# Order of work around an encoder's matmuls: operands, silu and residual ahead of weight casts, x turned between the first products, low parts on one engine

## The chip, the core and the metric

The kernel runs on one core of a Trainium2 chip. The core has five engines that run their own instruction queues in order: TensorE (PE, the matmuls and the transposes), VectorE (DVE), ScalarE (ACT), GpSimd (POOL) and SyncE (SP, here only the issuer of transfers). Operands lie in SBUF, products accumulate in PSUM, which has eight banks of 128 x 512 floats. The metric is the device time of one execution in microseconds (us).

## The reference

Two layers on x of 256 tokens by 1024 columns, all in float32. Each layer is

```python
x = x + 0.5 * swiglu(rms_norm(x, ffn1_norm[l]), ffn1_w_gate[l], ffn1_w_up[l], ffn1_w_down[l])
proj = rms_norm(x, mix_norm[l]) @ w_in[l]            # qa ka va qb kb vb, 2304 columns
out_a = windowed_gqa_sink(...)                       # 8 query heads, 2 key heads, ALiBi, sink
out_b = rms_norm(differential_attention(...), diff_subln[l]) * (1.0 - lam_init)
x = x + concat([out_a, out_b]) @ w_out[l]
x = x + 0.5 * swiglu(rms_norm(x, ffn2_norm[l]), ffn2_w_gate[l], ffn2_w_up[l], ffn2_w_down[l])
```

with `swiglu(h) = (silu(h @ w_gate) * (h @ w_up)) @ w_down` and 2816 hidden columns; a last RMSNorm ends it. All weights are read once, 167.5 MB of reads in the profile.

## The kernel before, in words

**Products in three parts.** A float32 product is made of three faster ones: every operand is split into a high part (rounded to float32r) and a low part (the rest), and high x high, low x high and high x low are added up in PSUM. So each weight tile is loaded to a buffer `raw` (SP issues the transfer), ACT writes the high part `whi` (line 106) and DVE the low part `wlo` (line 108). There are three buffers of each kind, and `weights()` starts the loads and casts of what comes two loads later (`LOOK = 2`). A load is 1 MB: 24 products of 512 columns use it. In the attention stage, from the fifth load of a layer on (`pooled`), the second half of each load's low parts is made by POOL instead of DVE. The products are lines 317 to 319 (`tokens`: the operand from x is the stationary side, 512 weight columns move) and 338 to 340 (`narrow`: the weights are stationary, 256 tokens move).

**Stages.** Each layer is feed-forward 1, attention, feed-forward 2. In a feed-forward the hidden columns come in five groups of 512 and one of 256. A group is a gate product and an up product (two loads each), `hidden` (silu of the gate on ACT, line 379, times up on DVE, line 384), `turn` (transposes on TensorE, line 398, then `split` into high on ACT, line 323, and low on DVE, line 324), and the product with the down weights, one group later. In the first group of a stage gate and up products alternate. In attention, `first_groups` makes the keys of the second head group, then come queries (`q_finish`), scores, softmax, transposes of the weights of attention, values, and the output projection.

**Between the stages.** `Residual.add` adds the result to x (`xk`, line 368) and takes the sum of squares on ACT (line 175). `Residual.turn(h)` turns half h of x: `Norm.pair` does four transposes (line 181) for two of the eight chunks of x and then two operands, high on ACT (line 185) and low on DVE (line 186). Half 0 is turned inside the last products of a stage, half 1 in `late()`, which the next stage calls in the middle of its first products. `stats` makes the factor of the norm from the sums of squares (DVE, POOL, DVE); it scales results, not operands, so that products can start without it. In the attention stage `spread` needs it, in the feed-forwards the silu.

**The start.** SP issues the four pieces of x in one queue with the pieces of the first two weight loads: x, two of each weight, x, two of each weight, x, x, and then the third load. `take_x` turns x in two halves, before the first and the second half of the first products.

**What orders the work.** The framework's scheduler orders each engine's instructions: of those that are ready in its model of time, the one written first goes first. A cast for the load after next is written before the products and operands of the present one, since `weights()` writes it, so it goes first where both are ready. On the chip each engine then keeps that order.

Of the kernel before, what the change touches and what calls it, by code (L numbers as in the profile page):

```python
# [33 lines left out]
def trunk(ctx: ExitStack, tc: tile.TileContext, x, n1, g1, u1, d1, nm, w_in, sink,  # L34
# [29 lines left out]


# [3 lines left out]
    pooled = set()  # L69
# [11 lines left out]
    def emit_load(i):  # L81
# [13 lines left out]
        for a, b in zip(cuts, cuts[1:]):  # L95
            if n == D:
                views = [(t[0][:, a:b, c:c + 512], t[1][:, a:b, c:c + 512], t[2][:, a:b, c:c + 512])
                         for t in [(raw, hi, lo)] for c in (0, 512)]
            elif i not in paired:
                views = [(raw[:, a:b], hi[:, a:b], lo[:, a:b])]  # L100
            else:
                views = [(raw.rearrange("p k (s c d) -> p c k s d", s=2, c=2)[:, c, a:b],
                          hi.rearrange("p k (c s d) -> p c k s d", s=2, c=2)[:, c, a:b],
                          lo.rearrange("p k (c s d) -> p c k s d", s=2, c=2)[:, c, a:b]) for c in range(2)]
            for r_, h_, l_ in views:
                act.copy(h_, r_)  # L106
                eng = pool if i in pooled and a in cuts[2:] else dve
                eng.tensor_tensor(l_, r_, f(h_), op=ALU.subtract)  # L108
            if i < 2:
                yield  # L110
# [11 lines left out]
    for l in range(DEPTH):  # L122
# [28 lines left out]
        pooled.update(range(mixed + 4, len(specs)))  # L151
# [14 lines left out]
    class Norm:  # L166
# [6 lines left out]
        def squares(self, t, c, n):  # L173
            j_ = tmp("junk", 2, (P, 512))
            self.last = act.activation(j_[:, :n], xk[:, t, c:c + n], AF.Square, accum_out=self.ss[:, t, c // 256:c // 256 + 1])

        def pair(self, j):
            sl = halves(bank())
            for i in range(2):
                for t in range(2):  # L180
                    pe.transpose(sl[:, i, t * P:(t + 1) * P], xk[:, t, (2 * j + i) * P:(2 * j + i + 1) * P], ident)
            xs = blk()
            for i in range(2):
                g = gcol[:, self.g0 + 2 * j + i:self.g0 + 2 * j + i + 1]
                act.activation(xs[:, i, 0:S], sl[:, i], AF.Identity, scale=g)  # L185
                dve.scalar_tensor_tensor(xs[:, i, S:512], in0=sl[:, i], scalar=g, in1=f(xs[:, i, 0:S]),  # L186
                                         op0=ALU.mult, op1=ALU.subtract)
# [27 lines left out]
    for j in range(4):  # L215
        sp.dma_start(xk[:, :, j * 256:(j + 1) * 256], x[0].rearrange("(t p) d -> p t d", p=P)[:, :, j * 256:(j + 1) * 256])
        for e in early * 2 if j < 2 else ():
# [142 lines left out]
    class Residual:  # L360
# [5 lines left out]
        def add(self, h, t):  # L366
            xv = xk[:, t, h * 512:(h + 1) * 512]
            dve.tensor_tensor(xv, xv, self.accs[h][t], op=ALU.add)
            self.nxt.squares(t, h * 512, 512)

        def turn(self, h):
            for j in (2 * h, 2 * h + 1):
                self.nxt.pair(j)

    def ffn(norm, aside=None, before=None, final=False):
        def gate(acc, t):
            g = tmp().rearrange("p a n -> p (a n)")
            n = acc.shape[1]
            act.activation(g[:, :n], acc, AF.Silu, scale=norm.r[:, t:t + 1])  # L379
            return g[:, :n]  # L380

        def up(h, acc, g, t):
            n = acc.shape[1]
            dve.scalar_tensor_tensor(h[:, t, :n], in0=acc, scalar=norm.hr[:, t:t + 1], in1=g, op0=ALU.mult, op1=ALU.mult)  # L384
# [7 lines left out]
        def turn(hs, n):  # L392
            out_ = []
            for i in range(n):
# [5 lines left out]
                split(hb, sl)  # L400
# [51 lines left out]
    def ffn_close(parts, nxt):  # L452
# [11 lines left out]
        def late():  # L464
            res.turn(1)
            nxt.stats()
        nxt.late = late

    def mix(l, norm, nxt_norm):
# [15 lines left out]
        def q_finish(sl, sc):  # L485
            t = tmp()
            q = tp.tile([P, 2, 512], F32R, tag="q", bufs=3, name=nm_("q"))
            for i in range(2):
                dve.scalar_tensor_tensor(t[:, i], in0=sl[:, i], scalar=sc[i], in1=norm.R, op0=ALU.mult, op1=ALU.mult)
            split(q, t)  # L490
# [118 lines left out]
        oa = [bank() for _ in range(2)]  # L609
# [10 lines left out]
        for h in range(HB):  # L620
            for t in range(2):
                j_ = tmp("junk", 2, (P, P))
                act.activation(j_, osl[t][:, h * P:(h + 1) * P], AF.Square, accum_out=ss[:, t, h:h + 1])
        d1 = den_b.rearrange("p h (t a) -> p a t h", a=2)[:, 0]
        dd = tmp("dd", 1, (P, 2, HB))
        dve.scalar_tensor_tensor(dd, in0=d1, scalar=EPS, in1=d1, op0=ALU.mult, op1=ALU.mult)
        dve.scalar_tensor_tensor(ss, in0=ss, scalar=1.0 / P, in1=dd, op0=ALU.mult, op1=ALU.add)
        rb = tmp("rb", 1, (P, 2, HB))
        pool.tensor_tensor(rb.rearrange("p t h -> p (t h)"), ss.rearrange("p t h -> p (t h)"), mhalf, op=ALU.pow)
        on = blk(F32)  # L630
        for t in range(2):
            dve.tensor_tensor(on[:, t].rearrange("p (h d) -> p h d", h=HB), osl[t].rearrange("p (h d) -> p h d", h=HB),
                              rb[:, t].unsqueeze(2).to_broadcast([P, HB, P]), op=ALU.mult)
# [18 lines left out]
        for hp, src in enumerate(turned(on)):  # L652
            dst = oT[2 + hp]
            act.activation(dst[:, :, 0:S], src, AF.Copy, scale=gsub[:, l:l + 1])
            dve.scalar_tensor_tensor(dst[:, :, S:512], in0=src, scalar=gsub[:, l:l + 1], in1=f(dst[:, :, 0:S]),
                                     op0=ALU.mult, op1=ALU.subtract)
# [28 lines left out]
        def late():  # L685
            res.turn(1)
            nxt_norm.stats()
        nxt_norm.late = late
# [93 lines left out]
```

## Time and profile before

| | before |
|---|---|
| median of three runs | 998.27 us (995.05 to 998.62) |
| the profiled execution | 997.01 us, span 995.2 us |
| TensorE busy | 961.8 us, 97% of the span |
| DVE, ACT, POOL busy | 550.0, 476.7, 53.6 us |
| mean granted TensorE clock | 0.991 |
| traffic | 169 GB/s over the span |

In the listings a line gives the start in us from the span's start, the length in us, engine, line of the kernel, operation, tile written and tiles read, shape and count; in brackets the idle time of the engine ahead of it and what ended that. In the waits a line gives the waiting engine and line, what it waited for, the total in us, how often and the longest. In the stretches each engine has its busy time and, in brackets, its instructions; then come the granted clock, the share of the DMA engines and GB/s. A busy TensorE is not one at its peak: lengths of neighbouring matmuls overlap, and the distance of their starts tells more.

### The profile page before, as it was taken

To read this page: it belongs to the slowest core of one execution; us is meant where nothing else is said; L and a number is where in the kernel's file an instruction comes from. 1 tells how busy PE (TensorE), PEld (TensorE's weight loads), DVE (VectorE), ACT (ScalarE), POOL (GpSimd) and SP (SyncE) were. 2 spreads that over 40 slices of the span, in tenths; PEclk is the share of its full clock that TensorE was granted. 3 is DMA by queue.
4 is the path that set the end of the run, shared out by engine and by line. 5 is a ranking of instruction groups with operands and counts; after the bars stand their busy time and mean duration, and the time that the engine had idled before them with its cause. 6 is when DMAs were issued, how large, how long until landed. Compare 5 with 4: busy or idle time off the path is not lost.

```text
span 995.2 us, 12394 instructions
## 1 busy us (share of the span) xinstructions
PE 961.8 (97%) x4940; PEld 813.7 (82%) x4940; DVE 550.0 (55%) x816; ACT 476.7 (48%) x809; POOL 53.6 (5%) x78
## 2 busy tenths in 40 slices
PE   6999999999999999999999999999999999999996
PEld 5788888889798788888878888887988887888885
DVE  4645454568945555454555545456597455454553
ACT  5544443457745443434445343435477355444433
POOL 4000000004100000000000000000230000000001
PEclk9999999999999999999999999999999999999999
DMA  8655565635515555656545565555445245565531
GB/s 264 212 195 186 174 206 173 204 97 182 150 43 169 178 202 172 196 182 200 181 143 194 172 209 170 192 188 184 118 142 152 85 169 169 190 212 187 195 127 42
DMA packets 98218, 169.39 MB, mean 170 GB/s; under 512 B 3182, under 2 KB 30896, under 8 KB 98160
## 3 DMA queue, kind: packets, MB, share of 16 engines
q1 hardware_dynamic: 97872, 168.31, 51.3%
q0 software_dynamic: 288, 0.30, 0.4%
q8 instruction: 38, 0.62, 0.2%
q14 instruction: 20, 0.16, 0.0%
HBM read 167.54 MB, written 1.05 MB: 169 GB/s over the span
## 4 chain that ended last, share of the span: by engine, by line
PE 90%; DVE 3%; ACT 3%; issue 2%; DMA 2%; SPq 0%; POOLq 0%; POOL 0%; ACTq 0%; DVEq 0%
PE ps L317 25%; PE ps L318 25%; PE ps L319 25%; PE ps L398 2%; PE ps L338 2%; PE ps L339 2%; PE ps L340 2%; DMA raw<-in_ffn_w_up_dram 2%; PE ps L615 1%; DVE wlo L108 1%; ACT whi L106 1%; PE ps L567 1%; PE ps L502 1%; ACT s L512 1%; PE ps L588 1%
## 5 line engine op out<-in xcount | busy, mean ns | idle before, releaser
L108 DVE TENSOR_TENSOR wlo<-raw,whi 128x1024 fp32r<-128x1024 f32 (+2 forms) x364 | 375.8, 1076 | 338.0 <-ACT whi L106 336.1
L106 ACT CAST whi<-raw 128x1024 fp32r<-128x1024 f32 (+2 forms) x392 | 323.2, 882 | 356.0 <-PE ps L318 322.4
L317 PE MATMUL ps<-whi,s 128*128 128x512 f32 x1126 | 433.2, 393 | 6.2 <-ACT s L185 5.3
L318 PE MATMUL ps<-whi,s 128*128 128x512 f32 x1126 | 439.0, 390 | 0.0
L319 PE MATMUL ps<-wlo,s 128*128 128x512 f32 x1126 | 437.0, 390 | 0.0
L317 PEld LDWEIGHTS ps<-whi,s 128*128 128x128 f32 x1126 | 211.8, 189 | 49.7 <-ACT s L185 5.8
L318 PEld LDWEIGHTS ps<-whi,s 128*128 128x128 f32 x1126 | 212.6, 189 | 43.8 <-DVE s L186 0.5
L319 PEld LDWEIGHTS ps<-wlo,s 128*128 128x128 f32 x1126 | 212.3, 189 | 43.5
L338 PE MATMUL ps<-s,whi 128*128 128x256 f32 x224 | 64.8, 293 | 4.3 <-ACT s L185 4.3
L339 PE MATMUL ps<-s,whi 128*128 128x256 f32 x224 | 64.9, 290 | 0.0
L340 PE MATMUL ps<-s,wlo 128*128 128x256 f32 x224 | 64.4, 288 | 0.0
L379 ACT ACTIVATE tmp<-ps,r 128x512 f32<-128x512 f32 (+1 forms) x48 | 31.2, 651 | 62.9 <-PE ps L319 62.8
L384 DVE SCALAR_TENSOR_TENSOR s<-ps,hr,tmp 128x512 f32<-128x512 f32 (+1 forms) x48 | 32.7, 705 | 41.2 <-PE ps L319 24.7
L338 PEld LDWEIGHTS ps<-s,whi 128*128 128x128 f32 x224 | 43.5, 196 | 5.6 <-ACT s L185 4.8
L339 PEld LDWEIGHTS ps<-s,whi 128*128 128x128 f32 x224 | 44.3, 198 | 0.1
L340 PEld LDWEIGHTS ps<-s,wlo 128*128 128x128 f32 x224 | 44.3, 198 | 0.0
L196 POOL TENSOR_TENSOR r<-ms,mhalf 128x2 f32<-128x2 f32 x6 | 4.2, 706 | 637.7 <-DVE ms L194 637.7
L512 ACT ACTIVATE s<-s,negm 128x256 f32<-128x256 f32 x64 | 31.8, 499 | 12.4 <-DVE negm L510 12.3
L324 DVE TENSOR_TENSOR s<-ps,s 128x512 fp32r<-128x512 f32 x48 | 31.0, 684 | 8.2 <-ACT s L323 8.2
L108 POOL TENSOR_TENSOR wlo<-raw,whi 128x256 fp32r<-128x256 f32 (+1 forms) x28 | 31.7, 1156 | 62.4 <-ACT whi L106 62.4
L323 ACT CAST s<-ps 128x512 fp32r<-128x512 f32 x48 | 25.7, 583 | 12.1 <-PE ps L398 9.7
L398 PE MATMUL ps<-ident,s 128*128 128x128 f32 x176 | 24.7, 274 | 4.3 <-DVE s L384 4.3
(115 smaller groups left out, 456.4 us busy)
## 6 DMA issues: line engine op xcount, KB each, us to landing
raw<-in_ffn_w_down_dram SPq DMA_DIRECT2D x44, 1024.0 KB, 4.9
raw<-in_ffn_w_gate_dram SPq DMA_DIRECT2D x39, 1024.0 KB, 5.0
raw<-in_ffn_w_up_dram SPq DMA_DIRECT2D x39, 1024.0 KB, 5.0
raw<-in_w_in_dram SPq DMA_DIRECT2D x14, 1024.0 KB, 5.1
raw<-in_ffn_w_gate_dram SPq DMA_DIRECT2D x8, 512.0 KB, 3.7
raw<-in_ffn_w_up_dram SPq DMA_DIRECT2D x8, 512.0 KB, 4.7
raw<-in_w_in_dram SPq DMA_DIRECT2D x8, 512.0 KB, 4.6
raw<-in_w_out_dram SPq DMA_DIRECT2D x4, 1024.0 KB, 4.8
```

Source lines behind the costliest of these rows:

```text
L106: act.copy(h_, r_)
L108: eng.tensor_tensor(l_, r_, f(h_), op=ALU.subtract)
L317: pe.matmul(accs[t], lhsT=xh, rhs=hi[:, k], start=kk == first, stop=False)
L318: pe.matmul(accs[t], lhsT=xl, rhs=hi[:, k], start=False, stop=False)
L319: pe.matmul(accs[t], lhsT=xh, rhs=lo[:, k], start=False, stop=kk == (last if isinstance(last, int) else last[t]))
L338: pe.matmul(acc, lhsT=wh, rhs=xv[:, 0:S], start=first and i == 0 and j == 0, stop=False)
L339: pe.matmul(acc, lhsT=wh, rhs=xv[:, S:512], start=False, stop=False)
L340: pe.matmul(acc, lhsT=wl, rhs=xv[:, 0:S], start=False, stop=last and i == len(kcs) - 1 and j == 1)
L379: act.activation(g[:, :n], acc, AF.Silu, scale=norm.r[:, t:t + 1])
L384: dve.scalar_tensor_tensor(h[:, t, :n], in0=acc, scalar=norm.hr[:, t:t + 1], in1=g, op0=ALU.mult, op1=ALU.mult)
L398: pe.transpose(sl[:, c, t * P:(t + 1) * P], hs[:, t, (2 * i + c) * P:(2 * i + c + 1) * P], ident)
L512: act.activation(e[:, t, c], e[:, t, c], AF.Exp, scale=-1.0, bias=negm[:, n:n + 1], accum_out=den[:, n:n + 1])
```

## The change

`urgent()` puts the instructions written inside it 300 places earlier in the order that the scheduler goes by. It is put around the operands of a norm (`Norm.operands`), the residual add, silu and the multiply with up, the split of the turned hidden block and the finish of the queries. The casts of weights do not get it.

The sums of squares leave `add` and follow `turn`, without priority. `late` gets a step number: the second half of x is turned after the first 24 products of a stage (one quarter of the 256-column products, the first half of the first pair of loads), before it was after the first half of all; the statistics come one step later. In a feed-forward's first group the second half of the gate product is finished before the second half of the up product. In the second group the turn of the first hidden block comes after the first 24 products of the gate.

At the start ACT's queue issues the four pieces of x, one after every two pieces of weights as written; x is turned in four steps between products, and the sums of squares of x queue behind the operands on ACT. The block that writes the attention constants was queued behind the last sum of squares on ACT and is now queued behind the last operand on DVE.

In attention the norm of the second head group (`norm_b`) with its transposes is written ahead of the last quarter of the first head group's products, before it was behind them. No low part of a weight is made on POOL any more: 28 operations of POOL, 12 of 512 and 16 of 256 columns, go to DVE.

```diff
+    def urgent():
+        return tc.high_priority(300)
...
-                eng = pool if i in pooled and a in cuts[2:] else dve
-                eng.tensor_tensor(l_, r_, f(h_), op=ALU.subtract)
+                dve.tensor_tensor(l_, r_, f(h_), op=ALU.subtract)
...
-            self.last = act.activation(j_[:, :n], xk[:, t, c:c + n], AF.Square, accum_out=...)
+            act.activation(j_[:, :n], xk[:, t, c:c + n], AF.Square, accum_out=...)
...
+            with urgent():
+                self.operands(j, sl)
+
+        def operands(self, j, sl):
             xs = blk()
             for i in range(2):
                 g = gcol[:, self.g0 + 2 * j + i:self.g0 + 2 * j + i + 1]
-                act.activation(xs[:, i, 0:S], sl[:, i], AF.Identity, scale=g)
-                dve.scalar_tensor_tensor(xs[:, i, S:512], ...)
+                self.last_act = act.activation(xs[:, i, 0:S], sl[:, i], AF.Identity, scale=g)
+                self.last = dve.scalar_tensor_tensor(xs[:, i, S:512], ...)
...
     for j in range(4):
-        sp.dma_start(xk[:, :, j * 256:(j + 1) * 256], ...)
-        for e in early * 2 if j < 2 else ():
+        act.dma_start(xk[:, :, j * 256:(j + 1) * 256], ...)
+        for e in early:
             next(e)
...
     def take_x(k):
-        if k < 2:
-            for j in (2 * k, 2 * k + 1):
-                norm.pair(j)
-                for e in early * 2 if k == 0 else ():
-                    next(e)
+        if k < 4:
+            norm.pair(k)
+            for e in early * 2 if k < 2 else ():
+                next(e)
         else:
-            for t in range(2):
-                for h in range(2):
-                    norm.squares(t, h * 512, 512)
+            with tc.issue_after(norm.last_act.ins):
+                for t in range(2):
+                    for h in range(2):
+                        norm.squares(t, h * 512, 512)
+            norm.stats()
...
         for k in range(0, KC, 2):            # first_groups
-            if k == 4:
-                norm.late()
+            if k:
+                norm.late(k // 2 + 1)
...
         def add(self, h, t):
             xv = xk[:, t, h * 512:(h + 1) * 512]
-            dve.tensor_tensor(xv, xv, self.accs[h][t], op=ALU.add)
-            self.nxt.squares(t, h * 512, 512)
+            with urgent():
+                dve.tensor_tensor(xv, xv, self.accs[h][t], op=ALU.add)
 
         def turn(self, h):
             for j in (2 * h, 2 * h + 1):
                 self.nxt.pair(j)
+            for t in range(2):
+                self.nxt.squares(t, h * 512, 512)
+
+        def late(self, k):
+            if k == 2:
+                self.turn(1)
+            elif k == 3:
+                self.nxt.stats()
...
-        for k0 in (0, 4):                    # ffn, first group
-            if before is not None:
-                before(k0 // 4)
-            elif k0 == 4:
-                norm.late()
-            ws = (weights(), weights())
-            for k in (0, 2):
-                for sl, w in zip((gs, us), ws):
-                    tokens(sl, norm.xs, w, k0, (k, k + 1))
-        if before is not None:
-            before(2)
-            norm.stats()
+        if before is None:
+            before = norm.late
+        before(0)
+        ws = (weights(), weights())
+        for k in (0, 2):
+            before(k // 2 + 1)
+            for sl, w in zip((gs, us), ws):
+                tokens(sl, norm.xs, w, 0, (k, k + 1))
+        before(3)
+        for sl in (gs, us):
+            tokens(sl, norm.xs, weights(), 4)
+        before(4)
         h = hidden(gs, us)
         for g in range(1, NGRP):
-            hT = turn(h, 2)
-            gs, us = [bank(), bank()], [bank(), bank()]
-            for sl in (gs, us):
-                for k0 in (0, 4):
-                    tokens(sl, norm.xs, weights(), k0)
+            if g > 1:
+                hT = turn(h, 2)
+            gs = [bank(), bank()]
+            tokens(gs, norm.xs, weights(), 0)
+            if g == 1:
+                hT = turn(h, 2)
+            tokens(gs, norm.xs, weights(), 4)
+            us = [bank(), bank()]
+            for k0 in (0, 4):
+                tokens(us, norm.xs, weights(), k0)
...
+            with urgent():                   # q_finish; likewise gate, up, split in turn
+                for i in range(2):
+                    dve.scalar_tensor_tensor(t[:, i], in0=sl[:, i], scalar=sc[i], in1=norm.R, ...)
+                split(q, t)
...
         for t in range(2):
             for c in range(4):
+                if (t, c) == (1, 2):
+                    norm_b()                 # the block below, and turned(on) with its operands
                 for a in range(2):
                     for kc in range(2):
                         pe.matmul(oa[t][...], lhsT=pT[c][...], rhs=vA[...], ...)
-        ss = tmp("ss", 1, (P, 2, HB))
-        ... squares of osl, mean, pow on POOL, on = osl * rb
-        for hp, src in enumerate(turned(on)):
-            ...
```

More of the change, by code (lines that the diff above doesn't have):

```diff
@@ L68, in trunk @@
     paired = set()
-    pooled = set()
     fine = {2, 3}
@@ L378, in gate @@
             n = acc.shape[1]
-            act.activation(g[:, :n], acc, AF.Silu, scale=norm.r[:, t:t + 1])
+            with urgent():
+                act.activation(g[:, :n], acc, AF.Silu, scale=norm.r[:, t:t + 1])
             return g[:, :n]
@@ L383, in up @@
             n = acc.shape[1]
-            dve.scalar_tensor_tensor(h[:, t, :n], in0=acc, scalar=norm.hr[:, t:t + 1], in1=g, op0=ALU.mult, op1=ALU.mult)
+            with urgent():
+                dve.scalar_tensor_tensor(h[:, t, :n], in0=acc, scalar=norm.hr[:, t:t + 1], in1=g, op0=ALU.mult, op1=ALU.mult)
         def hidden(gs, us):
@@ L399, in turn @@
                 hb = blk()
-                split(hb, sl)
+                with urgent():
+                    split(hb, sl)
                 out_.append(hb)
@@ L462, in ffn_close @@
             res.add(1, t)
[L464 to L467, printed above, removed]
+        nxt.late = res.late
     def mix(l, norm, nxt_norm):
@@ L487, in q_finish @@
             q = tp.tile([P, 2, 512], F32R, tag="q", bufs=3, name=nm_("q"))
-            for i in range(2):
-                dve.scalar_tensor_tensor(t[:, i], in0=sl[:, i], scalar=sc[i], in1=norm.R, op0=ALU.mult, op1=ALU.mult)
-            split(q, t)
+            with urgent():
+                for i in range(2):
+                    dve.scalar_tensor_tensor(t[:, i], in0=sl[:, i], scalar=sc[i], in1=norm.R, op0=ALU.mult, op1=ALU.mult)
+                split(q, t)
             return [q[:, 0], q[:, 1]]
@@ L616, in mix @@
                                   rhs=vA[:, kc, a * 64:a * 64 + 64], start=kc == 0, stop=kc == 1)
-        ss = tmp("ss", 1, (P, 2, HB))
[L620 to L633, printed above, removed]
         ra = tmp("ra", 1, (P, 4, 4))
@@ L683, in mix @@
             res.add(1, t)
[L685 to L688, printed above, removed]
+        nxt_norm.late = res.late
     fss = const.tile([P, 2, 4], F32, name="fss")
```

48 lines of the change are left out of this document (32 added, 16 removed).

## The prediction

> **What bounds the kernel now.** I read the page first, then the time listing of TensorE, then the waits, the listings of ACT, DVE and POOL around each TensorE hole, and last the stretches with their granted clock.
>
> ```profile
> PE 961.8 (97%) x4940; PEld 813.7 (82%) x4940; DVE 550.0 (55%) x816; ACT 476.7 (48%) x809; POOL 53.6 (5%) x78
> PE 90%; DVE 3%; ACT 3%; issue 2%; DMA 2%; SPq 0%; POOLq 0%; POOL 0%; ACTq 0%; DVEq 0%
> ```
>
> TensorE is the chain; nothing in the change takes work from it. In the listing 512-column products start 0.2275 us apart (140.03, 140.26, 140.49), 256-column ones 0.12, transposes 0.109. The middle of each feed-forward stage runs at that distance without a hole. So only time that neighbouring starts stand apart beyond this can be won. Added up over the trace, such excess is some 33 us net, and most of it lies in a dozen places. The waits say on whom:
>
> ```profile
> PEld ps L317 <- ACT s L185: 5.8, 2, 3.6
> PEld ps L338 <- ACT s L185: 4.8, 2, 2.4
> PEld ps L502 <- DVE q L324: 4.5, 2, 2.2
> PE ps L398 <- DVE s L384: 4.3, 4, 1.6
> ```
>
> Three of the four are products waiting for their own operands from ACT or DVE, and the fourth is the transpose of the hidden block waiting for silu times up. What ACT does meanwhile, at the start of the first attention stage (eight transposes began at 202.90, the product waits until 206.09):
>
> ```profile
> 202.87 1.66 ACT L106 CAST whi<-raw 128x512 fp32r<-128x512 f32 x3
> 204.44 0.62 ACT L175 ACTIVATE junk<-xk 128x512 f32<-128x512 f32 x1
> 204.97 0.18 ACT L175 ACTIVATION_READ_ACCUMULATOR junk<-xk 128x1 f32 x1
> 205.06 0.60 ACT L106 CAST whi<-raw 128x512 fp32r<-128x512 f32 x1
> 205.57 0.46 ACT L185 ACTIVATE s<-ps,gcol 128x256 fp32r<-128x256 f32 x1
> ```
>
> Four casts of a load two ahead and a sum of squares stand before the operand. Behind such a hole the clock falls:
>
> ```profile
> 25.80:29.30 3.50, 3.29 (x7) 2.32 (x8) 3.50 (x9) 2.77 (x5) 0.00 (x0) 0.51 0.96 304
> 204.00:208.00 4.00, 1.92 (x11) 1.92 (x12) 3.87 (x10) 3.73 (x11) 0.71 (x1) 0.85 0.40 129
> 208.00:212.00 4.00, 4.00 (x28) 4.00 (x27) 2.33 (x8) 1.63 (x4) 0.00 (x0) 0.73 0.92 250
> 252.00:256.00 4.00, 2.13 (x19) 1.80 (x17) 4.00 (x5) 3.33 (x7) 2.95 (x2) 1.00 0.00 0
> 504.00:508.00 4.00, 4.00 (x17) 3.53 (x16) 3.00 (x8) 2.24 (x6) 0.62 (x1) 0.61 0.79 262
> ```
>
> The last but one number before the bandwidth is the granted clock, ahead of the DMA share. From 206.8 to 210.2 starts are about twice as far apart (0.215 for 0.12): 3.4 us at half speed loses 1.7. The same follows the holes at 22, 500 and 691, not the one at 253.
>
> **The change part by part.** The profiled execution took 997.0 us (span 995.2), 1.3 below the median 998.3; the sum is made against 997.0.
>
> *Operands first, second half of x turned after the first products, residual add first.* Stages start badly three times: holes of 2.31 (203.7), 2.13 (500.5) and 2.31 (691.3), each with 1.7 of half clock behind it: 6.75 + 5.1 = 11.9. With priority the operand (0.46 on ACT, 0.48 on DVE) starts when its transposes end, and the adds no longer stand behind low parts (200.79 for three adds, after 2.36 of low parts). Turning the first half then fits under the twelve last products of the stage, 2.7. The second half comes after 24 products, 2.9 (256 columns) or 5.5 us (512); the last add, 0.69, and a transpose fit under that. Nearest row for a well covered start: the second feed-forward, 311 to 317, with 0.2 of excess. Bounds: an operand still behind one cast (1.05) leaves about 1.3 of each hole and the clock drop, gain 2.7; all of it, 11.9. I take 11.9 less 3 x 0.2 = **11.3**. The sums of squares lose their early place: 2 x 0.8 on ACT, then DVE, POOL (0.70) and DVE, in all some 3 us, needed at the end of the first group 11 us later, so nothing; without that cover it would be those 3 us per stage.
>
> *Start of the kernel.* x leaves SP's queue for ACT's: four issues of 0.44 to 0.62, 2 us, stand before ACT's table load (1.28) and its first cast at 4.19, so 0.7 + 2 + 1.28 just fits; bound a loss of 0.5. SP's ninth weight issue moves up by the four it loses. The last x piece was issued at 6.3 and landed 11.6 later; now it goes some 4 us sooner. The constants' DVE work (four operations, 2.2 us, 8.87 to 13.4) now queues behind the last DVE operand. The hole after the transposes at 21.6 is 3.54, then 1.7 of half clock: 5.2. Weights allow it: the third load's first low part ends at 21.9, and the fourth load's at 27.4, where its products would begin at 22.5 + 24 x 0.2275 = 27.9. An operand made on the spot costs 0.3. Bounds: 4.4 (late ACT) to 6.3 (first product at 7 instead of 9.15: five half-clock products, 1.1). I take **4.9**.
>
> *Gate finished before up, the next group's first 24 products before the turn.* Silu now follows the gate half, 24 products = 5.5 us before up ends; table load, two silus and two multiplies are 1.28 + 2 x 0.69 + 2 x 0.74 = 4.1, and another 5.5 us of products lie before the transposes. So these holes go: 1.03 (38.4), 0.46 (527), 1.74 (334.9) and 1.74 (822.5), **5.0**. Bounds 3 to 5. PSUM holds: silu frees the gate's two banks before the next two are asked for.
>
> *q first, no low parts on POOL.* The hole at 253.9 (2.18; again 2.19 at 741):
>
> ```profile
> 251.97 2.97 POOL L108 TENSOR_TENSOR wlo<-raw,whi 128x512 fp32r<-128x512 f32 x2 [6.67 <-ACT whi L106]
> 252.36 3.13 DVE L108 TENSOR_TENSOR wlo<-raw,whi 128x512 fp32r<-128x512 f32 x2
> 255.42 0.68 DVE L324 TENSOR_TENSOR q<-tmp,q 128x512 fp32r<-128x512 f32 x1
> ```
>
> q's low part waits behind two weight low parts that take 3.13 beside POOL, while two took 1.28 at 256.8 without it. Priority removes the hole; then DVE is the danger. POOL's work per layer becomes 8 x 0.36 + 6 x 0.64 = 6.7 us on DVE; overlap with POOL had cost DVE 5.5 there (2.06 at 242.5, 1.85 at 252.4, the rest at 224, 229 and 233). Net 1.2 into a stretch, 220 to 264, in which DVE was busy 39.9 of 44. Bounds: without the relief 6.7 - 4.1 idle = 2.6 lost per layer; with all, 2.2 won. I take half the hole, 2 x 1.2 = **2.4**, because the softmax operations right behind have no priority.
>
> *Norm of the second head group before the last quarter of the first group's products.* The hole at 287.9 (0.61, twice) is the output projection waiting for ACT's 0.70. The normed block ends at 285.4, three quarters of the 64 products at 280.2 + 5.3 = 285.5; the last 16 (1.8 us) cover the operand. **1.2**; bounds 0 and 1.2.
>
> Sum: 11.3 + 4.9 + 5.0 + 2.4 + 1.2 = 24.8; 997.0 - 24.8 = **972.2**.
>
> **The rivals.**
>
> *Half of it: the wait is passed on.* Behind operands stand the casts, behind q the softmax, and the cores run in order: an operand caught behind one running cast of 1.05 keeps the clock drop. Stage starts 2.7 to 5, start 3, gates 4, q nothing, norm 0.6: about 13, 984. For it: DVE busy 39.9 of 44. Against: the second feed-forward's start works with the same helper.
>
> *The clock still drops.* The half-clock stretches stay though the holes go: the stage starts give 3 x 1.7 = 5.1 less, 977. For it: a hole of 2.2 us cost clock at 203 and none at 253. Against: every stretch begins within 5 us of a hole that follows eight transposes (0.87), and the hole at 253 follows none. [...]
>
> *The order does not change*, because the scheduler had nothing else ready, or the operands were already first. Then 997. Against: the listing shows casts ahead of operands that were ready.
>
> *Slower: casts lose their lead.* An urgent silu, split or add set early into ACT's or DVE's queue waits for TensorE, and the casts behind it wait too. It costs nothing while a cast keeps its lead: a cast freed at 140.7 has its low part at 144.1, and its products begin at about 152.3, 8 us later. It decides from the point where each of the 24 groups of the four feed-forwards loses 24.8 / 24 = 1.0 us, that is, where casts come 9 us late; at 10 us late, 24 x 2 = 48 less 24.8, about 1020. Against: in the middle of a stage ACT sits idle 2.5 to 4 us before nearly every pair of casts.
>
> **How the numbers follow.** Forecast (966 to 976) 0.54; clock still drops (977) 0.06; half of it (980 to 988) 0.22; order unchanged 0.06; slower 0.08; better, with the first product and q at their upper bounds, 997.0 - 28.2 = 969 and less, 0.04. The range runs from 965, a little under that bound, to the far end of the half case, 988; the rest leaves it with 0.06 + 0.08 and a few hundredths. A measurement of this kernel tells about 0.5%, 5 us, from no change. Faster by more: 0.54 + 0.06 + 0.22 + 0.04 = 0.86; same 0.06; slower 0.08.
>
> **What would show it.** Right: no product waiting over 0.5 us for an operand of line 185 at the three stage starts, granted clock 1.00 in all stretches after the start, transposes of the hidden block directly behind products, first group done near 33 instead of 38, no POOL low parts, DVE near 550 + 13.4 - 11 = 552 busy. Wrong: products waiting for the casts or low parts of weights, the spreading product waiting for late squares, DVE without idle time around 250, a half-clock stretch that stays.

## The result and the profile after

| | before | after |
|---|---|---|
| median (four runs each) | 998.03 us (995.05 to 998.62) | 979.51 us (978.32 to 980.62) |
| ratio after / before | | 0.9821, 95% interval 0.9804 to 0.9837 |
| the profiled execution | 997.01 us, span 995.2 | 978.65 us, span 976.8 |
| mean granted TensorE clock | 0.991 | 0.996 |

The change saves 18.4 us in the profiled executions, where 24.8 were forecast; 972.2 was the forecast, inside a range of 965 to 988. The size is near, but one large term failed and two others came out differently. Lines of the kernel have moved: 185 is now 190 (operand, high part), 186 is 191, 181 is 182 (transposes of x), 106 and 108 are 109 and 110 (cast and low part), 317 to 319 are 323 to 325, 338 to 340 are 344 to 346, 398 is 415.

The page after, busy time and the shares of the chain that ended last:

```profile
PE 954.5 (98%) x4940; PEld 809.3 (83%) x4940; DVE 549.9 (56%) x844; ACT 475.7 (49%) x809; POOL 21.2 (2%) x50
PE 95%; DMA 2%; ACT 2%; issue 0%; DVE 0%; SPq 0%; POOLq 0%; POOL 0%; ACTq 0%
```

DVE took POOL's 28 low parts and is no busier (549.9 for 550.0). The waits of TensorE after, total in us, how often, longest:

```profile
PE ps L233 <- DMA grow<-in_ffn_norm_dram: 6.5, 1, 6.5
PE ps L344 <- ACT s L190: 4.3, 2, 2.1
PE ps L323 <- ACT s L190: 2.0, 1, 2.0
PE ps L323 <- ACT s L658: 0.9, 2, 0.5
PE ps L628 <- ACT v L617: 0.6, 2, 0.3
```

The wait for silu times up and the wait for q are gone. The three waits for the first operand of a stage (line 190) are not. The fourth row is the one that was to go with the norm of the second head group, and the fifth is new.

Where the 18.8 us up to the last product came from is read by setting the starts of the same TensorE operations (the landmarks) in the two traces against each other. Each row is the change of that difference over a stretch.

| stretch, by its ends | after minus before, us | the prediction's term |
|---|---|---|
| start to the hidden block's transposes in group two (73.31, now 66.02) | -7.29 | start -4.9, first gate -1.03 |
| the three later first groups of feed-forwards: 309.88 to 370.51, 499.77 to 561.3, 797.51 to 858.14 | -1.83, -0.54, -1.83 | gates -1.74, -0.46, -1.74 |
| attention stages' starts to first scores (202.90 to 232.15; 690.56 to 719.77) | -1.49, -1.45 | stage starts, with the one at 500: -11.3 |
| first scores to products of the second head group (to 276.5; to 764.12) | -2.76, -2.80 | q -2.4 |
| from there to the next transposes of x (309.88; 797.51) | +0.50, +0.73 | norm -1.2 |

The loss in the last row does not come from the move of the norm, as two of the experiments below show: all but 0.2 of it comes with POOL's low parts going to DVE. So it belongs with the row above it, and the two together are -4.3 over both layers.

**The stage starts.** ACT after, at the first attention stage (start, length, line, operation, tiles, shape, count):

```profile
194.86 0.61 ACT L176 ACTIVATE junk<-xk 128x512 f32<-128x512 f32 x1
195.59 2.18 ACT L109 CAST whi<-raw 128x512 fp32r<-128x512 f32 x4
197.68 0.62 ACT L176 ACTIVATE junk<-xk 128x512 f32<-128x512 f32 x1
198.30 0.45 ACT L190 ACTIVATE s<-ps,gcol 128x256 fp32r<-128x256 f32 x1
```

TensorE beside it:

```profile
195.62 1.03 PE L182 MATMUL ps<-ident,xk 128*128 128x128 f32 x8
198.81 0.51 PE L344 MATMUL ps<-s,whi 128*128 128x256 f32 x2 [2.15 <-ACT s L190]
```

It is the picture of before: four casts and a sum of squares stand ahead of the operand. The excess between neighbouring starts is 2.31 (196.4), 2.13 (487.7) and 2.31 (677.9), to 10 ns the three holes of before. What the stages won, 1.5 each, is a half-clock stretch that no longer follows the first and the third hole; it still follows the second:

```profile
491.20:494.60 3.40, 3.40 (x13) 2.92 (x12) 2.84 (x8) 2.16 (x6) 0.61 (x1) 0.50 0.90 282
677.90:682.00 4.10, 1.95 (x17) 1.71 (x16) 3.98 (x10) 4.10 (x12) 0.56 (x1) 1.00 0.53 176
```

The number ahead of the DMA share is the granted clock: 0.50 behind the hole of 2.13, 1.00 through the longer hole of 2.31.

**The queries.** DVE after, at the place where two low parts had taken 3.13 beside POOL:

```profile
245.76 2.49 DVE L110 TENSOR_TENSOR wlo<-raw,whi 128x512 fp32r<-128x512 f32 x4
248.17 0.68 DVE L330 TENSOR_TENSOR q<-tmp,q 128x512 fp32r<-128x512 f32 x1
```

Four low parts in 2.49 are 0.62 each, for 1.57 each before. q still stands behind them; they are only shorter, and TensorE runs from product to product.

**The second head group.** TensorE after, around the end of attention:

```profile
265.86 3.39 PE L628 MATMUL ps<-v,s 128*128 128x128 f32 x28 [0.28 <-ACT v L617]
269.09 7.03 PE L670 MATMUL ps<-vA,s 128*128 128x64 f32 x62
275.96 0.39 PE L635 MATMUL ps<-ident,s 128*128 128x128 f32 x2
276.36 0.82 PE L635 MATMUL ps<-ident,s 128*128 128x128 f32 x6
277.63 1.19 PE L323 MATMUL ps<-whi,s 128*128 128x512 f32 x4 [0.45 <-ACT s L658]
```

`norm_b` is written ahead of the last 16 of the 64 products of the first head group (line 670), but 62 of them went ahead of its transposes (line 635), so that nothing covers the operand (line 658) and its hole of 0.61 stays. A new hole stands ahead of the second head group's values. ACT there, after:

```profile
262.49 0.67 ACT L617 ACTIVATE v<-ps,r 128x512 f32<-128x512 f32 x1
263.05 2.17 ACT L109 CAST whi<-raw 128x512 fp32r<-128x512 f32 x4
265.13 0.68 ACT L617 ACTIVATE v<-ps,r 128x512 f32<-128x512 f32 x1
```

And before, the same three steps of ACT and the products that read the values:

```profile
273.39 0.69 ACT L596 ACTIVATE v<-ps,r 128x512 f32<-128x512 f32 x1 [0.31 <-PE ps L590]
273.97 2.17 ACT L106 CAST whi<-raw 128x512 fp32r<-128x512 f32 x4
276.05 0.68 ACT L596 ACTIVATE v<-ps,r 128x512 f32<-128x512 f32 x1
276.50 3.74 PE L607 MATMUL ps<-v,s 128*128 128x128 f32 x32
```

In both, the second copy of the values waits behind four casts; the order is an old one. Before, the copy ended at 276.73, 0.23 after the first of the products. Now it ends at 265.81, 0.84 after the first (264.97), because TensorE, no longer held up ahead of q, comes sooner. So the products that read it (line 628) have a hole of 0.45 (0.50 in the second layer).

### The profile page after: what moved, and what is told of

Read it like the earlier page. It is cut to its first block, busy times and chain, and to the rows that moved or that the text cites. A ratio compares the mean times of both kernels' runs of the same rounds, so it can differ in the third digit from the quotient of the medians.

```text
span 976.8 us, 12379 instructions
## 1 busy us (share of the span) xinstructions
PE 954.5 (98%) x4940; PEld 809.3 (83%) x4940; DVE 549.9 (56%) x844; ACT 475.7 (49%) x809; POOL 21.2 (2%) x50
## 4 chain that ended last, share of the span: by engine, by line
PE 95%; DMA 2%; ACT 2%; issue 0%; DVE 0%; SPq 0%; POOLq 0%; POOL 0%; ACTq 0%
PE ps L323 26%; PE ps L324 26%; PE ps L325 26%; PE ps L344 3%; PE ps L345 3%; PE ps L346 3%; PE ps L415 2%; DMA raw<-in_ffn_w_gate_dram 2%; PE ps L670 1%; PE ps L523 1%; ACT whi L109 1%; PE ps L609 1%; PE ps L610 1%; PE ps L611 1%; PE ps L628 1%; PE ps L182 1%
## 5 line engine op out<-in xcount | busy, mean ns | idle before, releaser
L344 PE MATMUL ps<-s,whi 128*128 128x256 f32 x224 | 63.3, 287 | 4.3 <-ACT s L190 4.3
L345 PE MATMUL ps<-s,whi 128*128 128x256 f32 x224 | 63.6, 285 | 0.0
L344 PEld LDWEIGHTS ps<-s,whi 128*128 128x128 f32 x224 | 42.4, 191 | 5.3 <-ACT s L190 4.8
L345 PEld LDWEIGHTS ps<-s,whi 128*128 128x128 f32 x224 | 42.9, 192 | 0.2
L190 ACT ACTIVATE s<-ps,gcol 128x256 fp32r<-128x256 f32 x48 | 20.7, 472 | 7.4 <-PE ps L182 4.1
L415 PEld LDWEIGHTS ps<-ident,s 128*128 128x128 f32 x176 | 20.7, 140 | 3.2
```

The costliest lines, as they stand in the source:

```text
L344: pe.matmul(acc, lhsT=wh, rhs=xv[:, 0:S], start=first and i == 0 and j == 0, stop=False)
L345: pe.matmul(acc, lhsT=wh, rhs=xv[:, S:512], start=False, stop=False)
L415: pe.transpose(sl[:, c, t * P:(t + 1) * P], hs[:, t, (2 * i + c) * P:(2 * i + c + 1) * P], ident)
```

## The experiments

The kernel before has a median of 996.7 us beside the first four runs (12 runs of it) and 996.5 beside the last four (7 runs). Holes are, as in the prediction, the excess of the distance between two neighbouring starts.

**The first casts and the squares queued behind the stage's operands.** The changed kernel, with an order written out on ACT in both kinds of stage:

```diff
-        ws = (weights(), weights())
+        with tc.issue_after(norm.last_act.ins):
+            ws = (weights(), weights())
...
-            for t in range(2):
-                self.nxt.squares(t, h * 512, 512)
+            with tc.issue_after(self.nxt.last_act.ins):
+                for t in range(2):
+                    self.nxt.squares(t, h * 512, 512)
```

> The changed kernel, with the casts of the first loads of a stage and the sums of squares queued on ACT behind the high parts of the operands of the first half of x (an order edge, no wait). Theory A, the holes at the stage starts stayed because four casts and a sum of squares still stand ahead of the operand in ACT's queue: the holes of 2.31, 2.13 and 2.31 us shrink to about 0.6 each, the half-clock stretch behind the second one goes (1.7), 3 x 1.6 + 1.7 = 6.5 us less than the changed kernel, 973. Rival B, the operand is late because the closing products of both halves end together and the residual adds come last: the holes stay above 1.5, and the time is 977 to 980.

Measured 971.29 us (970.69 to 971.76), 0.9736 of before (0.9719 to 0.9753): 8.2 below the changed kernel. ACT and TensorE of this kernel at the first attention stage:

```profile
196.01 0.84 ACT L190 ACTIVATE s<-ps,gcol 128x256 fp32r<-128x256 f32 x2 [4.21 <-PE ps L182]
```

```profile
195.69 0.60 PE L182 MATMUL ps<-ident,xk 128*128 128x128 f32 x4
196.53 0.51 PE L344 MATMUL ps<-s,whi 128*128 128x256 f32 x2 [0.24 <-ACT s L190]
```

ACT now stands idle until the operand can be made, and all three holes are 0.40. From 10.2 to 965.9, behind the last product, the profile of this kernel has no half clock. It is a little better than theory A. So the forecast of 11.3 for the stage starts was the right price: 2.9 came with the change by the clock alone, and the landmarks of this kernel show another 2.0, 3.4 and 2.0 at the three starts, 10.3 together. What failed is that the change would bring that order.

**The priority taken away.** `urgent()` returns an empty context; the rest of the change stays.

```diff
-        return tc.high_priority(300)
+        return ExitStack()
```

> The changed kernel with the priority taken away (urgent() returns an empty context); everything else of the change stays. Theory A, the priority decides nothing here, because at the stage starts the casts are placed before the operands for another reason (in the scheduler's time model the operand is ready later than on the chip): same time as the changed kernel, 979.5 within 1, holes at the three stage starts again 2.31, 2.13 and 2.31, no hole over 1 at the q products. Rival B, the priority is what closed the holes of 2.2 at the q products and brought silu and multiply forward: those holes come back, 2 x 2.2 plus half clock, 983 to 988.

Measured 980.13 us (977.68 to 980.59; 0.983 of before, 0.9815 to 0.9844), the changed kernel's time. The holes are 2.31, 2.13 and 2.31 again, and none at q. ACT at the first stage start of this kernel:

```profile
194.80 2.18 ACT L109 CAST whi<-raw 128x512 fp32r<-128x512 f32 x4
196.89 0.63 ACT L176 ACTIVATE junk<-xk 128x512 f32<-128x512 f32 x1
197.51 0.45 ACT L190 ACTIVATE s<-ps,gcol 128x256 fp32r<-128x256 f32 x1
```

Theory A holds: with priority and without it, ACT does the same work in the same order here, 0.79 earlier in this trace because its start was. More than that: TensorE, ACT and POOL run the same sequence of lines and tiles in the two traces from the first instruction to the last, and on DVE six of 844 places differ, all of them around the finish of a query block. So the priority was at work, but not where the holes are. The edit that gave the change its name is worth nothing that these runs can tell. A reason that fits the listing of after was not tested by itself: the casts start at 195.59, 0.03 before the first transpose that the operand needs. When ACT comes free, the casts are ready and the operand is not. A priority chooses among what is ready; it keeps no engine idle for what is about to be.

**Only the casts queued behind the operands**, the squares left where they were:

```diff
-        ws = (weights(), weights())
+        with tc.issue_after(norm.last_act.ins):
+            ws = (weights(), weights())
```

> The changed kernel with only the casts of the stage's first weights queued behind the stage's first operands on ACT; the sums of squares stay where they were. Theory A, the four casts carry the hole and the squares a smaller part: the holes of 2.31, 2.13 and 2.31 go to between 0.8 and 1.3, since up to three squares of 0.62 now stand ahead of the operand; no half-clock stretch follows; 973 to 976. Rival B, the squares alone are enough to keep the operand late, because they wait for the last residual add: holes stay at 1.7 or more, 977 to 980. Rival C, the squares cost nothing: 0.4 as with both held, 971.

Measured 971.01 us (970.61 to 972.25), 0.9745 (0.9731 to 0.976), with holes of 0.40: rival C, the squares cost nothing. ACT of this kernel at the first stage start:

```profile
195.03 0.64 ACT L176 ACTIVATE junk<-xk 128x512 f32<-128x512 f32 x1
195.91 0.47 ACT L190 ACTIVATE s<-ps,gcol 128x256 fp32r<-128x256 f32 x1 [0.15 <-PE ps L182]
```

Three sums of squares stand ahead of the operand and end before its transposes do. The four casts alone made the hole.

**The low parts on POOL put back** into the changed kernel, priority kept:

```diff
-                dve.tensor_tensor(l_, r_, f(h_), op=ALU.subtract)
+                eng = pool if i in pooled and a in cuts[2:] else dve
+                eng.tensor_tensor(l_, r_, f(h_), op=ALU.subtract)
```

> The changed kernel with the second half of the low parts of the later attention loads made by POOL again. Theory A, it was POOL's slowing of DVE that made q late, so its removal closed the hole ahead of the scores: the hole of 2.2 us comes back in both layers, about 984. Rival B, the new order closed it: within 1 us of the changed kernel, 980.

Measured 987.53 us (987.30 to 988.13), 0.9900 (0.9883 to 0.9917), 8.0 more than the changed kernel. DVE, and one stretch behind the hole, of this kernel:

```profile
245.81 3.13 DVE L112 TENSOR_TENSOR wlo<-raw,whi 128x512 fp32r<-128x512 f32 x2
248.87 0.68 DVE L333 TENSOR_TENSOR q<-tmp,q 128x512 fp32r<-128x512 f32 x1
```

```profile
251.20:254.70 3.50, 3.50 (x14) 3.03 (x13) 3.50 (x14) 2.56 (x9) 0.00 (x0) 0.51 1.03 236
```

The 3.13 is back, and with it holes of 2.18 and 2.46 ahead of the q products, although q's finish has its priority. This time a half clock follows each, which the same hole in the kernel before did not bring, and so the time lies above the 984 of theory A. The hole of 0.45 at the second copy of the values is gone here, with the norm still written early: from the first products of the second head group to those of the first, the landmarks are where they were before (0.00 in both layers; after has +0.54 and +0.78).

**The low parts on DVE, and nothing else**, in the kernel before:

```diff
-        pooled.update(range(mixed + 4, len(specs)))
```

> The kernel before with one edit: no low parts on POOL, all on DVE. Theory A, the shared pair of low parts (3.13 beside POOL, 1.28 alone) is what made q late: the holes of 2.18 and 2.19 ahead of the q products shrink under 1 in both layers without any priority, gain 2 x 2 = 4, so some 993, plus or minus 2 by the half-clock stretches that fall or do not fall. Rival B, the 6.7 of POOL's work per layer makes DVE the bound in the q, k, v stretch (39.9 of 44 busy before): other products wait there for low parts, no gain or a loss up to 5, 997 to 1002.

Measured 989.58 us (988.34 to 990.92), 0.993 (0.9914 to 0.9947), 6.9 less than before from one removed line. DVE and TensorE at the first q of this kernel:

```profile
251.85 0.68 DVE L108 TENSOR_TENSOR wlo<-raw,whi 128x512 fp32r<-128x512 f32 x1
252.45 0.68 DVE L323 TENSOR_TENSOR q<-tmp,q 128x512 fp32r<-128x512 f32 x1
```

```profile
253.01 0.28 PE L339 MATMUL ps<-s,wlo 128*128 128x256 f32 x1
253.22 0.50 PE L501 MATMUL ps<-s,q 64*128 64x256 f32 x4
```

The q holes are gone in both layers without any priority: 4.4 by the holes. It is below the 993 of theory A, because in the profiled execution two half clocks (503.7 and 694.9 before) do not occur: 3.4 more, together 7.8; the last product of the trace stands 8.0 earlier. The holes ahead of those two are still there, so the 3.4 is luck of that execution.

The landmarks of this kernel split the row of q: from the first scores to the second head group they move by -2.75 and -2.77, as in after, and then by +0.55 and +0.55 up to the first products of the first head group. The hole is there too, with the old order of the norm:

```profile
274.22 3.39 PE L606 MATMUL ps<-v,s 128*128 128x128 f32 x28 [0.28 <-ACT v L595]
```

So the low parts alone give what after has in both rows, but for 0.2 in the second layer.

**Gate before up and the later turn alone**, on the kernel before:

```diff
+        for sl in (gs, us):
+            tokens(sl, norm.xs, weights(), 4)
...
-            hT = turn(h, 2)
+            if g > 1:
+                hT = turn(h, 2)
+            gs = [bank(), bank()]
+            tokens(gs, norm.xs, weights(), 0)
+            if g == 1:
+                hT = turn(h, 2)
```

> The kernel before, with only the order of the feed-forward changed: second half of the gate product before that of up, first 24 products of the second group before the turn of the first hidden block. If the gate holes were won by this order alone (1.03 + 0.46 + 1.74 + 1.74): 5.0 us under the kernel before, 993. Rival, that the priority of silu and split is needed: the holes stay at half or more, 996 to 998.

Measured 990.92 us, but from 986.47 to 995.83 over nine runs; 0.9944 (0.9922 to 0.9965). The four holes ahead of the hidden block's transposes are gone, so the order alone closes them and the rival falls; it is as in the changed kernel, where at 329.31 and 329.54 product and transposes follow each other at 0.23. In this kernel's profile the hole at the start is 4.36 long, for 3.54, and two half-clock windows follow it for one, so that part of the gain is spent there.

**x issued by SP as before**, the rest of the change kept:

```diff
-        act.dma_start(xk[:, :, j * 256:(j + 1) * 256], ...)
-        for e in early:
+        sp.dma_start(xk[:, :, j * 256:(j + 1) * 256], ...)
+        for e in early * 2 if j < 2 else ():
```

> The changed kernel with the four pieces of x issued by SP again, between the weight pieces as before. Theory A, the start was won by x landing early: the last pieces land after 15 us again, the products of the second half wait for their operands at about 22, and the start loses 4 to 5 us, about 984. Rival B, it was won by turning x in four steps and by the late squares: within 1 us of the changed kernel.

Measured 983.26 us (981.93 to 984.16), 0.9855 (0.9836 to 0.9874), 3.7 more than the changed kernel. TensorE of this kernel, and then of the changed one:

```profile
9.28 1.12 PE L182 MATMUL ps<-ident,xk 128*128 128x128 f32 x4 [3.02 <-DMA xk<-in_x_dram]
10.04 0.78 PE L323 MATMUL ps<-whi,s 128*128 128x512 f32 x1
```

```profile
6.49 0.26 PE L233 MATMUL ps<-ident,grow 16*128 16x16 f32 x1 [6.49 <-DMA grow<-in_ffn_norm_dram]
6.67 1.97 PE L182 MATMUL ps<-ident,xk 128*128 128x128 f32 x8
8.35 1.91 PE L323 MATMUL ps<-whi,s 128*128 128x512 f32 x4
```

Neither theory is right as written. The hole at 22 is gone in both, so what stays of the change at the start removes it: x turned in four steps, the late squares or the constants' work behind the operands, which no run takes apart. ACT's queue lets the first product start 1.7 earlier. By the landmark in group two that queue is worth 2.5 (68.48 for 66.02). The two profiled executions stand 5.5 apart, because this one has three half clocks after the first rise and after has one. In after the last thing awaited at the start is not x but the row of constants `grow`.

**What is left, taken together.** The changed kernel with casts and squares held as in the first experiment, the second copy of the values ahead of the next casts, the last quarter of the first head group's products queued behind the transposes of the second, and that row of constants on SP's queue:

```diff
+            v_last = act.activation(vB[:, t], vsl[t], AF.Copy, scale=norm.r[:, t:t + 1])
+        with tc.issue_after(v_last.ins):
+            ahead(nxt[0] - 1)
...
+                  with tc.issue_after(last_turn[0].ins) if last_turn[0] is not None else ExitStack():
                     for kc in range(2):
...
-    pool.dma_start(grow1, n1.rearrange("l (k p) -> (l k) p", p=P))
+    sp.dma_start(grow1, n1.rearrange("l (k p) -> (l k) p", p=P))
```

> The changed kernel with casts and squares queued behind the operands at the stage starts, the second v copy ahead of the casts of the next loads, the last quarter of the output products queued behind the transposes of the second head group, and the first row of constants loaded by SP's queue in place of POOL's. Theory A, each wait left is the one named: the holes of 0.45 at the v copy and 0.61 at the second group's operand go in both layers (2.1), and 0.8 at the start if the transposes no longer wait for that constant: 971.3 less 2 to 3 = 968 to 969.5. Rival B, the waits pass on (the casts now late for the output projection, or the start bound by the x transfers): 971 or more.

Measured 968.58 us (968.21 to 969.07), 0.9719 of before (0.9705 to 0.9734): the best kernel here, 10.9 below the changed one. TensorE at the second head group:

```profile
266.02 5.47 PE L683 MATMUL ps<-vA,s 128*128 128x64 f32 x48
271.33 1.25 PE L647 MATMUL ps<-ident,s 128*128 128x128 f32 x8
272.41 1.90 PE L683 MATMUL ps<-vA,s 128*128 128x64 f32 x16
274.12 1.17 PE L327 MATMUL ps<-whi,s 128*128 128x512 f32 x4
```

48 products, the transposes, 16 products, and no wait ahead of the output projection: with the order written out, the norm's step does what the prediction said of it. Both holes are gone in both layers. Against the first experiment's kernel the attention stages are each 0.5 shorter in the landmarks, about half of their 2.1 us. Most of the other half is in the landmark itself: 91 products of the output projection stand ahead of the next transposes of x here, and 89 there, and two products are 0.46. Up to the second group of the next feed-forward only another 0.16 to 0.18 of that comes out, since a new hole of 0.25 (297.53) follows the transposes. The first product comes at 7.16 for 8.55 there, which is worth only 0.2 in group two, so the step at the start is worth less than the 0.8 that was put on it. The time is that of theory A.

## Why the prediction was right, and where it was wrong

It was right in sign and range. Its sum was 6.0 too large against the 18.8 of the landmarks: stage starts 8.4 and norm 1.2 too large, start, gates and q together 3.6 too small. The total is as near as it is because the second group makes up for part of the first, and 2.9 of it came by the clock.

**Stage starts, 11.3: the failed step, 2.9.** The sentence "With priority the operand starts when its transposes end" is what fell. The priority changed nothing (980.13 without it), the casts kept their place, and the holes stayed to 10 ns. The price was right (10.3 with the order written out). The rival "the order does not change" was true at this place, and the reason that it named, that nothing else was ready, fits the listing. It had a chance of 0.06 because I took the listing's casts ahead of the operand for a choice between two ready instructions. The listing of before already spoke against it: the first cast began at 202.87 and the eight transposes at 202.90. The counter-example, the start of the second feed-forward, is no such case: there ACT's casts end at 310.7, it stands idle for 0.83 until the transposes are done, and products of the stage before lie between the transposes.

**The rest of that term, the clock.** The 2.9 that came are two half-clock stretches that fell away while their holes stayed. That is luck: the kernel without priority has the same order on TensorE and ACT, and in its profile the half clock stays behind the third hole, not the second. The prediction took each stretch as the price of its hole. The section on the hardware shows behind which holes they came.

**Start, 4.9: 6.3** (7.29 less the first gate's 1.03), the upper bound given. ACT's four issues (2.02) and its table load (1.28) are in the trace as worked out and cost nothing. The first product gained 0.8 (8.35), and the hole at 22 and its half clock are gone altogether. The first group's products end near 32.5, as was to be seen ("near 33"): its transposes begin at 37.93, behind 24 products of the next group.

**Gates, 5.0: 5.2** (1.0 and 4.2). Right in place and size.

**q, 2.4: 4.4**, the upper bound given: 5.6 in its own stretch, less the 1.1 that the low parts cost behind it, at the second copy of the values. The cause was right that two low parts beside POOL take 3.13, but "priority removes the hole" was wrong; POOL's leaving removed it (the kernel with one line removed has no such hole, the changed one with POOL put back has it). I took half of the hole for fear that DVE would be the bound. It was not: its busy time did not grow, since 28 more operations are paid for by shorter ones. What the prediction did not see is that ACT, not DVE, is next: TensorE comes sooner, and meets four casts ahead of a copy of values.

**Norm, 1.2: nothing.** The written order did not reach TensorE's queue, and the hole of 0.61 stayed. The +1.23 of the landmarks is the low parts' 1.1 and 0.2 more in the second layer that no run explains. The timing of the prediction held: POOL's power ended at 273.1, the multiply on DVE at 274.4, and by then (274.4 - 269.09) / 0.114 = 47 of the 64 products had started. But 62 products stand ahead of the transposes in TensorE's queue, and that order is made before the run. I had taken the order as written for the order on the engine.

**The rivals.** Half of it (984) named the right mechanism at one place, an operand caught behind casts that are already in the queue; it expected q to be lost, and that was won. The slower case did not occur: in after TensorE's waits for casts of weights add up to 0.3 us. The rival that the clock still drops never met its condition, holes that go, in the changed kernel; one half-clock stretch stayed, but behind a hole that stayed. Where the three holes did go, to 0.40 in the first experiment, no half clock was left.

## What to carry to other kernels

When an operand comes late because another instruction stands ahead of it, compare the times at which the two became ready. Where the other was ready first, priority did nothing here, and an order written out that keeps it back, on an engine with 51% to spare, was worth 8 us. Moving POOL's share of element-wise work to DVE cost DVE nothing here (549.9 us busy for 550.0), since a low part took DVE 1.57 beside POOL and 0.62 without: time the same operation alone and beside the other engine. And a gain that is made of half-clock stretches is not to be booked per hole: two traces of one order of work had it behind different holes.

## What the runs showed of the hardware

**In these profiles the half clock goes by a grid of time.** In all ten every half-clock stretch between the first rise and the end is 3.413 us long, or twice that, and begins at a whole number of such windows after the moment at which the clock first rose, to 0.002 of a window (3.4133 us): 13.65, 194.56, 491.52 and 682.67 us after it in before (4, 57, 144 and 200 windows), 481.28 in after (141). Whether a half clock followed a hole of TensorE over 1 us went with how much of the hole lay inside one window. The profiles of before, after and five experiments have 36 such holes after the first rise:

```
idle time of the hole inside one window     holes   followed by a half clock
2.01 us and more                               16      16
1.35 to 1.88 us                                16       1   (of 1.77)
under 1.35 us                                   4       0

hole, us into its window        profile                     half clock
0.42 to 2.73                    before, 203.7               yes
2.24 to 4.55 (1.18 and 1.13)    after, 196.4                no
1.84 to 4.15 (1.58 and 0.74)    without priority, 195.6     no
0.57 to 2.88                    POOL put back, 197.1        yes
```

All four of the second table are the same hole of 2.31 at the same place of the program. In the kernel without priority the one hole of the three that is followed by a half clock is the third, in after it is the second:

```profile
486.80:491.00 4.20, 2.24 (x17) 1.78 (x14) 3.96 (x8) 4.02 (x11) 0.68 (x1) 1.00 0.53 176
678.50:682.00 3.50, 3.50 (x19) 3.50 (x18) 3.44 (x12) 2.69 (x7) 0.69 (x1) 0.51 0.86 242
```

A half-clock stretch costs 1.7 us (3.41 at 0.50), so the time of a kernel with holes of 2 us can vary by up to that for each of them, from one execution to the next. The kernel with only the gate's part of the change, with six holes over 2 us, spread over 9.4 us in nine runs, and the granted clock of these went from 0.987 to 0.996 with it; 0.009 of 990 is 8.9 us. The three kernels with the stages' holes closed spread over 0.9 to 1.6 in four runs each. It need not vary: the kernel with POOL put back, with five such holes, spread over 0.8, at a clock of 0.991 each time. The idle time of the one hole does not settle it alone between 1.77 and 2.01, for one of 1.88 did not lower the clock and one of 1.77 did; no run says what else counts.

The first rise (products 0.43 apart ahead of it, 0.23 behind it) came 3.06 us after the first product in before (at 12.21) and 1.59 in after (at 9.94), and anywhere from 1.2 to 3.7 in the ten profiles. Against the rival that the clock still drops, the prediction had it that every stretch of before stands near a hole behind eight transposes (0.87). The transposes are not needed: the holes ahead of q follow products, and three of them (2.18 and 2.46 with POOL put back, 2.18 in the kernel with the gate's part alone) are followed by a half clock.

**DVE beside POOL.** A low part of 512 columns takes DVE 0.62 in a row of its own kind (2.49 for four) and 1.57 beside a like operation of POOL (3.13 for two), which itself takes about 1.5 (2.97 for two). Sharing a load's low parts between the two engines was slower than leaving them all to DVE: 3.13 for two on DVE with POOL's two beside them, 2.49 for all four on DVE alone. No run shows by what POOL slows DVE.
